# Priorities for the scan's chain and the merges of inverses in a hybrid encoder layer

## The chip, the core and the metric

The kernel runs on one core of a Trainium2 chip. A core has five engines that work side by side, each with a queue of its own that it takes strictly in order: TensorE (PE; its weight loads are shown as PEld), VectorE (DVE), ScalarE (ACT), GpSimd (POOL) and SyncE (SP). Transfers are issued from the queues of SP, POOL and ACT. The metric is the device time of one execution in microseconds (us). Three executions of the kernel before gave 2390.2, 2390.23 and 2392.87 us, a median of 2390.23.

## What is computed

One layer of a bidirectional hybrid encoder: a half-step feed-forward part, a mixing part and a second half-step feed-forward part, each with a residual, for 1024 tokens of width 1024. The mixing part has two groups of eight heads: a dilated attention and a recurrent delta rule that runs forward and backward over the tokens. The change touches the recurrence:

```python
def _rwkv7_step(state, inp):
    r, w, k, v, kk, kka = inp
    sa = jnp.einsum('dbhvk,dbhk->dbhv', state, kk)
    state = state * w[..., None, :] - sa[..., :, None] * kka[..., None, :] + v[..., :, None] * k[..., None, :]
    y = jnp.einsum('dbhvk,dbhk->dbhv', state, r)
    return state, y
...
for l in range(DEPTH):
    f = _swiglu(_rmsnorm(h, ffn1_pre_g[l]), ffn1_w_gate[l], ffn1_w_up[l], ffn1_w_down[l])
    h = h + 0.5 * _rmsnorm(f, ffn1_post_g[l])
    z = _rmsnorm(h, mix_pre_g[l]) @ w_in[l]
    y_att = _attention_group(z[..., :ATT_IN], cos, sin, attn_out_g[l])
    y_rwkv = _rwkv7_group(z[..., ATT_IN:], ...)
    mix = jnp.concatenate([y_att, y_rwkv], axis=-1) @ w_out[l]
    h = h + _rmsnorm(mix, mix_post_g[l])
    f = _swiglu(_rmsnorm(h, ffn2_pre_g[l]), ffn2_w_gate[l], ffn2_w_up[l], ffn2_w_down[l])
    h = h + 0.5 * _rmsnorm(f, ffn2_post_g[l])
```

## The kernel before

The recurrence is not run token by token. The tokens are cut into 8 blocks (`NB`) of two chunks of 64 tokens each, for both directions and all heads. Inside a chunk the recurrence becomes matrix products with the inverse of a triangular matrix, and only the chain of states goes from chunk to chunk. A block n passes four steps:

- `prep(n)`: loads the block's inputs (`in3`, `th_w`, `th_a`; SP, L182), forms scaled keys on DVE and ACT (`pr` L810 and L811, `bk` L814, L815 and L822, `th_a` L819 and L821), multiplies them on PE (`lp`, L830), masks the products on DVE (`lm`, L832), transposes keys (`bp` L838, copied to `bt` by ACT, L840) and writes parts of `lm` to a buffer in memory (`d_x`, SP, L846). Tile `in3` has one buffer.
- `solve(n)`: loads the right-hand side `X` from `d_x` (SP, L182) and inverts all 16-row triangles of the block at once, by 31 steps of two DVE instructions (`ttmp` L866, `Ti` L868); DVE copies the result into `X` (L870), and POOL writes `Ti` and `X` out (`d_t` L872, `d_tt` L873). POOL also clears the next `Ti` (L860, L862).
- `merge(n)`: POOL loads the small inverses back (`d11` L883, `tt` L886), and PE and ACT put inverses of full chunks together from them by two rounds of small products (`pa` L894, copy L896, `pb` L900, copy L902). `d11` has one buffer, `tt` two.
- `chain(n)`: for each of the two chunks, SP loads values into `uv` and into the state tile `sv` (L908; two buffers each), PE forms the right-hand side from the state (`xu` L941, copied to `xs` by ACT, L944), multiplies by the chunk's inverse (`xu` L952, copied to `uv` by ACT, L954), and from `uv` forms the new state (`st`, L949 and L959 to 960) and the output (`y`, L956 to 963). The profile names all sums that go through the helper `add` by its line, L937. DVE scales the state into the next `sv` (L968), and ACT copies `y` to `yb` (L970) and stores it (`y_d`, L972).

In the same loop, `project_attended` multiplies the output of the attention by the output weights: a load and a scaling on DVE (`yat` L1072), a transpose on PE (`yq` L1075), its high part on ACT (`yah` L1077) and remainder on DVE (`yal` L1078), 24 products for a tile on PE (`po`, L1064), and a copy and store on ACT (`yao` L1083). `out_weights` prepares the weights (`woh` L1054 on ACT, `wol` L1055 on DVE). After the loop, `finish_half` turns the outputs into rows of the mixing product (`f_y` L994, `yc` L995, `var` L1004, `bonus` L1011, `rstd` L1014, `gate` L1025).

The program is written in one sequence, and a scheduler then orders the instructions of each engine: among those that are ready by its model it takes the most urgent, and urgency is by default the place in the written sequence. Inside `tc.high_priority()` an instruction counts as more urgent than everything outside; with `offset=1000` it counts as written 1000 places earlier. What is fixed by this at build time is the order in each queue, and it is kept at run time even where an instruction waits.

## Time and profile before

| what | value |
|---|---|
| median of three executions | 2390.23 us |
| the profiled execution's own time | 2398.21 us |
| its span, from the first to the last instruction | 2396.4 us |
| PE busy | 2233.1 us (93%) |
| DVE busy | 1778.9 us (74%) |
| ACT busy | 1030.6 us (43%) |
| POOL busy | 572.8 us (24%) |
| TensorE clock, mean over the span | 0.951 |

The span is 1.8 us shorter than the execution's time; the rest lies around it. The loop of the scan takes the stretch from about 1269 to 1624 us: solve 0 has ended at 1268, and the last chain ends at 1623.6. Before it stand the first feed-forward part, the attention and the projections; behind it the finish, the mixing product and the second feed-forward part.

How the views are read: a busy share says how long an engine worked, not what it waited for. "DVE sv L968 <- PE st L937: 19.4, 9, 5.8" means that DVE stood idle for 19.4 us, nine times, 5.8 us at the longest, ahead of instructions of line 968 until PE's product for `st` was done. SPq is the queue of SyncE, that issues transfers. In a timeline, a row gives the start, the duration, the engine, line and operation, the tiles written and read, how many such instructions follow each other, and in brackets the idle time ahead of the row and what ended it. The granted clock is the share of full speed that TensorE was given.

### The profile page before, as it was taken

How to read it: one execution, taken by the hardware profiler on the slowest of the kernel's cores; microseconds unless marked ns; L12 is line 12 of the kernel's file. 1: busy time of each engine (PE TensorE's matmuls, PEld its weight loads, DVE VectorE, ACT ScalarE, POOL GpSimd, SP SyncE). 2: the span in 40 equal slices, each digit the busy share in tenths (PEclk: the TensorE clock that was granted, in tenths of full speed). 3: DMA queues.
4: the chain of work that ended last, by engine and by line, in shares of the span. 5: the costliest groups of instructions: out<-in, count | busy, mean ns of one | idle time of the engine just before them, and what ended most of it. 6: DMA issues, size and time to landing. Idle time of an engine off the chain costs nothing. (4 is left out here: it accounts for less than half of the span.)

```text
span 2396.4 us, 39330 instructions
## 1 busy us (share of the span) xinstructions
PE 2233.1 (93%) x14532; PEld 1801.5 (75%) x14532; DVE 1778.9 (74%) x2917; ACT 1030.6 (43%) x1918; POOL 572.8 (24%) x668
## 2 busy tenths in 40 slices
PE   6999999999999998999986788898989999999997
PEld 4788888788786676778775577775768888887886
DVE  8899999865675345666556766746889999997565
ACT  4422333354676304556544444445442233335452
POOL 6244344500000010111101121132234443442000
PEclk8999999999999998999995698789989999999999
DMA  5344544576743415322366766558534544448655
GB/s 155 110 172 150 171 158 156 181 257 194 227 152 133 161 50 157 84 71 72 91 173 174 177 157 166 146 173 268 186 107 172 180 150 167 164 152 268 194 189 180
DMA packets 359763, 386.03 MB, mean 161 GB/s; under 512 B 73618, under 2 KB 268050, under 8 KB 359572
## 3 DMA queue, kind: packets, MB, share of 16 engines
q1 hardware_dynamic: 311968, 284.82, 39.5%
q0 software_dynamic: 27248, 86.05, 9.7%
q10 hardware_dynamic: 20356, 12.66, 1.8%
q8 instruction: 114, 1.87, 0.3%
q14 instruction: 77, 0.63, 0.1%
HBM read 257.53 MB, written 125.89 MB: 160 GB/s over the span
## 5 line engine op out<-in xcount | busy, mean ns | idle before, releaser
L186 ACT ACTIVATE wh<-raw 128x512 fp32r<-128x512 f32 (+1 forms) x273 | 168.2, 627 | 261.8 <-DVE raw L62 94.0
L81 PE MATMUL gu<-xh,wh 128*128 128x512 f32 x704 | 277.2, 394 | 2.3 <-ACT wh L186 1.1
L187 DVE TENSOR_TENSOR wl<-raw,wh 128x512 fp32r<-128x512 f32 (+1 forms) x273 | 275.6, 1013 | 2.1 <-ACT wh L186 1.2
L81 PE MATMUL gu<-xh,wl 128*128 128x512 f32 x704 | 275.9, 392 | 0.0
L81 PE MATMUL gu<-xl,wh 128*128 128x512 f32 x704 | 275.7, 392 | 0.0
L415 PE MATMUL pd<-gl,gwh 128*128 128x512 f32 x616 | 240.5, 390 | 2.5 <-DVE gl L187 2.5
L415 PE MATMUL pd<-gh,gwh 128*128 128x512 f32 x616 | 239.6, 390 | 0.6 <-DVE row L86 0.6
L415 PE MATMUL pd<-gh,gwl 128*128 128x512 f32 x616 | 239.8, 389 | 0.0
L86 DVE TENSOR_TENSOR row<-gu,row 128x512 f32<-128x512 f32 x308 | 206.3, 682 | 26.1 <-PE gu L81 24.2
L187 DVE TENSOR_TENSOR gwl<-graw,gwh 128x512 fp32r<-128x512 f32 (+1 forms) x176 | 117.9, 672 | 128.4 <-ACT gwh L186 125.7
L116 POOL DMA_DIRECT2D d_hid<-row x154 | 84.7, 551 | 473.3 <-DVE row L114 446.2
L186 ACT ACTIVATE gwh<-graw 128x512 fp32r<-128x512 f32 (+1 forms) x176 | 101.4, 576 | 188.4 <-PE pd L415 157.5
L81 PEld LDWEIGHTS gu<-xh,wh 128*128 128x128 f32 x704 | 133.5, 190 | 31.6 <-ACT xh L186 2.0
L81 PEld LDWEIGHTS gu<-xl,wh 128*128 128x128 f32 x704 | 133.4, 189 | 27.5
L81 PEld LDWEIGHTS gu<-xh,wl 128*128 128x128 f32 x704 | 133.1, 189 | 27.6
L415 PEld LDWEIGHTS pd<-gl,gwh 128*128 128x128 f32 x616 | 115.6, 188 | 28.0 <-DVE gl L187 4.3
L415 PEld LDWEIGHTS pd<-gh,gwh 128*128 128x128 f32 x616 | 115.6, 188 | 25.3 <-DVE row L86 1.0
L415 PEld LDWEIGHTS pd<-gh,gwl 128*128 128x128 f32 x616 | 115.7, 188 | 23.8
L187 DVE TENSOR_TENSOR gl<-raw,gh 128x512 fp32r<-128x512 f32 x160 | 112.3, 713 | 17.0 <-ACT gh L186 16.7
L94 ACT ACTIVATE row<-row 128x512 f32<-128x512 f32 x44 | 27.8, 633 | 221.3 <-DVE row L86 217.5
L145 POOL TENSOR_TENSOR ws<-ws 128x512 f32<-128x512 f32 x88 | 114.2, 1298 | 1.1
L186 ACT ACTIVATE gh<-raw 128x512 fp32r<-128x512 f32 x160 | 98.0, 621 | 33.7 <-DMA raw<-in_ffn_w_down_dram 21.8
(354 smaller groups left out, 5345.7 us busy)
## 6 DMA issues: line engine op xcount, KB each, us to landing
d_hid<-row POOLq DMA_DIRECT2D x154, 256.0 KB, 2.4
graw<-d_hid SPq DMA_DIRECT2D x132, 256.0 KB, 3.0
raw<-in_ffn_w_gate_dram SPq DMA_DIRECT2D x88, 256.0 KB, 3.0
raw<-in_ffn_w_up_dram SPq DMA_DIRECT2D x88, 256.0 KB, 3.3
ws<-in_ffn_w_down_dram SPq DMA_DIRECT2D x88, 256.0 KB, 4.5
d_ws<-ws POOLq DMA_DIRECT2D x88, 256.0 KB, 2.3
raw<-d_ws SPq DMA_DIRECT2D x88, 256.0 KB, 2.7
raw<-in_ffn_w_down_dram SPq DMA_DIRECT2D x66, 256.0 KB, 3.6
```

The lines of the kernel that those rows point to most:

```text
L81: self.K.nc.tensor.matmul(ps, a[:, k, :], b[:, k, :], start=(k == 0 and i == 0), stop=(k == 3 and i == 2))
L86: add = lambda o, x: V.tensor_tensor(o, ps, x, op=OP.add)
L94: A.activation(y[:, 0], y[:, 0], AF.Silu)
L116: put = lambda n, y: G.dma_start(self.hid[n - 1, j // 2], y)
L145: G.tensor_tensor(o, a, b, op=OP.subtract)
L186: self.nc.scalar.activation(h, src, AF.Copy)
L187: (eng or self.nc.vector).tensor_tensor(l, src, h, op=OP.subtract)
L415: T.matmul(ps[x], a[:, ts], b, start=(m == 0 and k == 0), stop=(m == NM - 1 and k == 2))
```

## The change

The merge of every block but the first is written inside a priority of 1000 places, and the chain inside the highest priority. Nothing is added and nothing removed; the two lines that open these blocks shift later lines by two.

```diff
             for n in range(NB):
                 if n:
-                    self.merge(n, blk[n], sc, pm)
-                self.chain(n, blk.pop(n), sc, pc)
+                    with self.tc.high_priority(offset=1000):
+                        self.merge(n, blk[n], sc, pm)
+                with self.tc.high_priority():
+                    self.chain(n, blk.pop(n), sc, pc)
                 upto(n + 3)
                 for t in ([0, 1] if n == 0 else [n + 1] if n + 1 < NT else []):
                     self.project_attended(eo, sc, pe, t, WA, rs_a)
```

Every engine's order changes in the scan. Three places follow. First SyncE's queue at the solve of block 4, whose right-hand side is `X_13133`; `sv_13987` is a state tile of chain 3, `d_x0_152` the buffer through which block 4's `lm` goes. Before:

```order
L846 DMA d_x0_152<-lm_12991 32x16x32 x4
L908 DMA sv_13439<-d_vt_137 64x2x256 x2
L823 DMA d_kd0_140<-th_a_13543 128x4x128
L182 DMA X_13133<-d_x0_152 64x1024 x2
L908 DMA uv_13883<-d_vt_137 64x2x256 x2
L908 DMA sv_13886<-d_vt_137 64x2x256 x2
L182 DMA th_w_14089<-d_w0_110 128x4x128
L908 DMA uv_13984<-d_vt_137 64x2x256 x2
L182 DMA th_a_14091<-d_a0_116 128x4x128
L182 DMA yat_14304<-d_ya_101 128x512
L908 DMA sv_13987<-d_vt_137 64x2x256 x2
```

And now:

```order
L908 DMA uv_13883<-d_vt_137 64x2x256 x2
L823 DMA d_kd0_140<-th_a_13543 128x4x128
L182 DMA th_w_14089<-d_w0_110 128x4x128
L182 DMA th_a_14091<-d_a0_116 128x4x128
L908 DMA sv_13886<-d_vt_137 64x2x256 x2
L908 DMA uv_13984<-d_vt_137 64x2x256 x2
L846 DMA d_x0_152<-lm_12991 32x16x32 x4
L908 DMA sv_13987<-d_vt_137 64x2x256 x2
L182 DMA X_13133<-d_x0_152 64x1024 x2
```

The load of `X_13133` stood ahead of all values and states of chain 3 and now stands behind them, as does the store that it reads. At the start of the loop the same happens to the input `in3_11717` of block 1, second half; block 0's tiles are `uv_12212`, `sv_12215`, `sv_12218`, `uv_12296` and `sv_12299`. SyncE's difference there:

```order
-L182 DMA wor_12158<-in_w_out_dram 128x512
-L908 DMA uv_12212<-d_vt_137 64x2x256
-L182 DMA in3_11717<-d_rk_125 128x12x128
-L908 DMA uv_12212<-d_vt_137 64x2x256
+L908 DMA uv_12212<-d_vt_137 64x2x256 x2
 L908 DMA sv_12215<-d_vt_137 64x2x256 x2
 L908 DMA sv_12218<-d_vt_137 64x2x256 x2
 L908 DMA uv_12296<-d_vt_137 64x2x256 x2
-L908 DMA sv_12299<-d_vt_137 64x2x256
-L182 DMA wor_12164<-in_w_out_dram 128x512
-L908 DMA sv_12299<-d_vt_137 64x2x256
+L908 DMA sv_12299<-d_vt_137 64x2x256 x2
+L182 DMA in3_11717<-d_rk_125 128x12x128
+L182 DMA wor_12158<-in_w_out_dram 128x512
```

The input moved from behind the first load of values to behind the last load of a state. The third place is PE at merge 6 and the chunk of chain 6 behind it; `pa_15234` and `pb_15269` are the merge's products, `xu_15316` the chunk's right-hand side, `po_15526` and `po_15542` the attended products of the last tile. Before:

```order
L894 MATMUL pa_15234<-d11_15227,lm_14087 32x32 x32
L937 MATMUL st_15317<-sv_15083,ident_62 64x256 x4
L937 MATMUL y_15318<-pr_14098,sv_15083 64x64 x8
L937 MATMUL y_15318<-pr_14166,sv_15083 64x64 x8
L1064 MATMUL po_15526<-wol_12185,yah_15522 128x512
L1064 MATMUL po_15526<-woh_12184,yal_15523 128x512
L1064 MATMUL po_15526<-woh_12196,yah_15522 128x512
L900 MATMUL pb_15269<-tt0_11629,d11_15227 32x32 x32
L941 MATMUL xu_15316<-sv_15083,lm_14087 64x64 x16
```

And now:

```order
L894 MATMUL pa_15234<-d11_15227,lm_14087 32x32
L1064 MATMUL po_15542<-woh_12166,yah_15522 128x512
L1064 MATMUL po_15542<-wol_12167,yah_15522 128x512
L1064 MATMUL po_15542<-woh_12166,yal_15523 128x512
L1064 MATMUL po_15542<-woh_12178,yah_15522 128x512
L1064 MATMUL po_15542<-wol_12179,yah_15522 128x512
L941 MATMUL xu_15316<-sv_15083,lm_14087 64x64 x7
L1064 MATMUL po_15542<-woh_12178,yal_15523 128x512
L1064 MATMUL po_15542<-woh_12190,yah_15522 128x512
L900 MATMUL pb_15269<-tt0_11629,d11_15227 32x32 x32
```

All of `po_15526` has moved ahead of this merge, into and before chain 5, and only the 12 rows of `po_15542` are left beside chain 6, ahead of its first multiplication by the inverse; before, products of both stood in chain 6 up to its end. On POOL the loads of each merge (L883, L886) now stand ahead of the memset of the next `Ti` (L860, L862), and on PE merge 1 stands ahead of 12 attended products that it stood behind.

## The prediction

> **What bounds the kernel now.** The page comes first: where does TensorE (PE) lose time, and is its clock whole there?
>
> ```profile
> span 2396.4 us, 39330 instructions
> ...
> PE   6999999999999998999986788898989999999997
> ...
> PEclk8999999999999998999995698789989999999999
> ```
>
> A slice is 2396.4 / 40 = 59.9 us. The clock row is 9 nearly everywhere; slices 21 to 27 (1258 to 1677 us) hold its 5, 6, 7 and 8, and the PE row falls to 6 to 8 there. That is the scan of the recurrence, the stage that the change re-orders. Busy time in stretches of 100 us shows the same:
>
> ```profile
> 1200.00:1300.00 100.00, 75.84 (x578) 61.96 (x576) 58.91 (x128) 45.66 (x81) 12.42 (x19) 0.79 0.67 174
> 1300.00:1400.00 100.00, 75.91 (x923) 61.27 (x922) 71.35 (x224) 41.73 (x79) 15.61 (x26) 0.71 0.64 162
> 1400.00:1500.00 100.00, 87.19 (x1510) 72.51 (x1509) 65.97 (x172) 52.32 (x99) 15.66 (x26) 0.92 0.66 170
> 1500.00:1600.00 100.00, 91.89 (x1521) 74.31 (x1520) 68.35 (x224) 42.31 (x81) 21.91 (x33) 0.84 0.54 138
> ```
>
> Columns: stretch, length, busy us of PE, PE's weight loads, DVE, ACT and POOL, granted clock, DMA share, GB/s. No engine is full. PE at 76 to 92% runs partly on a reduced clock; DVE, which owns the solves, is at 59 to 71%. So the stage is bound by waits that go round between engines: prepare a block (PE and DVE), solve its 16-row inverses (DVE), merge them (PE and ACT), run the chain (PE, ACT, DVE). The table of waits for 1237 to 1640 us (total us, times, longest) says who waits:
>
> ```profile
> POOL d_t L872 <- DVE ttmp L866: 126.9, 2, 68.7
> ...
> DVE sv L968 <- PE st L937: 19.4, 9, 5.8
> DVE yal L1078 <- ACT yah L1077: 14.3, 4, 7.9
> ...
> DVE pr L810 <- DMA in<-d_rk: 8.0, 3, 6.1
> DVE ttmp L866 <- DMA X<-d_x: 7.4, 3, 4.6
> ...
> SPq L908 <- PE y L937: 59.7, 18, 10.8
> ```
>
> The first row is POOL idling until a solve is done, and costs nothing by itself. The four DVE rows do cost: the solver stands still for states, attended products and loads. The last row is the SyncE queue, held by a load of values into a state (sv) whose buffer the chain still reads. The last stage shows how such waits line up; here DVE, then PE:
>
> ```profile
> 1531.00 0.60 DVE L870 COPY X<-Ti 128x512 f32<-128x512 f32 x1
> ...
> 1551.04 0.60 DVE L870 COPY X<-Ti 128x512 f32<-128x512 f32 x1
> 1559.50 0.69 DVE L1078 TENSOR_TENSOR yal<-yq,yah 128x512 fp32r<-128x512 f32 x1 [7.86 <-ACT yah L1077]
> 1565.67 0.68 DVE L968 TENSOR_TENSOR sv<-st,gc 64x512 f32<-64x512 f32 x1 [3.33 <-PE st L937]
> ...
> 1584.03 0.60 DVE L870 COPY X<-Ti 128x512 f32<-128x512 f32 x1
> ```
>
> ```profile
> 1552.51 0.66 PE L1075 MATMUL yq<-ident,yat 128*128 128x128 f32 x4
> ...
> 1573.96 1.20 PE L894 MATMUL pa<-d,lm 32*32 32x32 f32 x64
> ...
> 1595.83 0.24 PE L894 MATMUL pa<-d,lm 32*32 32x32 f32 x2
> ...
> 1604.70 1.12 PE L995 MATMUL yc<-f_y,k_cen 128*128 128x512 f32 x2 [2.48 <-POOL f_y L994]
> ...
> 1623.55 1.13 PE L1025 MATMUL gate<-f_sg,g2w 128*128 128x256 f32 x4
> ```
>
> The L870 copies end the solves of blocks 5, 6 and 7 (at 1531.6, 1551.6, 1584.6). The solve of block 7 takes 33.0 us from the one before, because its owner waits 7.86 us for an attended product and 3.33 us for a state. The merges of blocks 6 and 7 start 22.4 us (1573.96 - 1551.6) and 11.2 us behind their solves, and chain 7 ends at 1623.55, where a finish unit's gate row takes PE.
>
> **The change part by part.** Nothing is added or removed; every term below is a shift. I walked the new order of every engine by hand with the durations of such groups (columns: total us, mean ns, idle before):
>
> ```profile
> L868 DVE TENSOR_TENSOR Ti<-Ti,ttmp 128x96 f32<-128x96 f32 (+20 forms) x248 | 61.1, 253 | 5.4
> ...
> L832 DVE TENSOR_TENSOR lm<-lp,k_tri 128x512 f32<-128x512 f32 x56 | 37.3, 684 | 15.5 <-PE lp L830 15.4
> ```
>
> *Part 1, the start.* SyncE now issues all values and states of block 0 before the input of block 1's second half, and the last of these waits for chain 0's first product. Now the input goes before them:
>
> ```profile
> 1270.44 0.78 SPq L182 DMA_DIRECT2D in<-d_rk  x1
> ...
> 1286.41 0.57 SPq L908 DMA_DIRECT2D sv<-d_vt  x1
> ```
>
> The held state load goes at 1286.41. In the new order PE's first chain product stands ahead of the preparation's, so I put that load near 1279 and the input near 1280, 10 us late; DVE's 6.1 us wait (its longest for `in`, in the table) is for this very load and hides none of it. But chain 0's rows, which held the preparations that follow, are then done, and the walk gives back 6 of the 10: **+4** for solve 1 (bounds 0 and +10).
>
> *Part 2, merge loads on POOL.* They stand ahead of the memsets for the next solve's tile:
>
> ```profile
> 1352.30 0.78 POOL L872 DMA_DIRECT2D d_t<-Ti  x1 [68.70 <-DVE ttmp L866]
> ...
> 1357.29 0.53 POOL L860 MEMSET Ti<- 128x512 f32 x1 [1.77 <-DMA d_t<-Ti]
> 1357.91 0.67 POOL L883 DMA_DIRECT2D d<-d_t  x1
> ```
>
> That alone is worth 0.53 us. On PE the merge of block 1 now also passes 12 attended products, ahead of which PE idles:
>
> ```profile
> 1354.84 0.79 PE L1064 MATMUL po<-woh,yah 128*128 128x512 f32 x1 [13.87 <-ACT woh L1054]
> ...
> 1370.54 0.31 PE L894 MATMUL pa<-d,lm 32*32 32x32 f32 x2
> ```
>
> Solve 1 ends at 1352.3 and its merge starts 18.2 us later, behind those products. The first merge load was issued at 1357.9, so the merge could start some 4 us after that (an estimate from the X load of part 3), near 1362. Chains 1 to 3 so run 10 to 15 us sooner. That moves no solve directly; it frees the blocks' buffers and the states.
>
> *Part 3, solve 4.* Its right-hand side (the X load) stands behind a state load that waits for chain 3. In the trace the X load goes first:
>
> ```profile
> 1426.75 1.10 SPq L182 DMA_DIRECT2D X<-d_x  x2
> ...
> 1450.73 1.24 SPq L908 DMA_DIRECT2D sv<-d_vt  x2
> ```
>
> ```profile
> 1434.23 0.19 DVE L866 TENSOR_TENSOR ttmp<-X,Ti 128x31 f32<-128x31 f32 x1 [4.56 <-DMA X<-d_x]
> ```
>
> The load of 1450.73 is the one it is now behind. It goes when chain 3's state product is read; with chain 3 some 15 us sooner that is about 1434 to 1435. From the X load's issue to the solve's first row the trace has 7.5 us (1434.23, after 4.56 us of idling), so solve 4 starts near 1441 to 1442, not 1434.2: **+7** (part 1's +4 goes into the same wait). Bounds: 0, and +25 if the state load goes at 1450.73 as now.
>
> *Part 4, preparations inside that wait.* While solve 4 waits, DVE has block 5's preparation ahead in its queue. One preparation is 8 masks of 0.684 us (the L832 row: 56 for seven blocks) and two each of the six products L810, L811, L814, L815, L821 and L822, whose rows have the shape and, to 0.01 us, the time of this one:
>
> ```profile
> L821 DVE TENSOR_TENSOR th_a<-th_a,in 128x512 f32<-128x512 f32 x13 | 9.0, 689 | 14.9 <-ACT th_a L819 14.9
> ```
>
> That is 8 x 0.684 + 12 x 0.689 = 13.7 us. Before, this was done after solve 4; the new order does nearly all of it first. Of the 13.7 I take 10, since its PE products also queue: **-10** (bounds 0 and -13.7). With part 3, solve 5 ends 3 us sooner; by the walk block 7's preparation is then also finished, where now DVE still does its last four masks after it:
>
> ```profile
> 1540.00 0.68 DVE L832 TENSOR_TENSOR lm<-lp,k_tri 128x512 f32<-128x512 f32 x1
> ...
> 1542.84 0.69 DVE L832 TENSOR_TENSOR lm<-lp,k_tri 128x512 f32<-128x512 f32 x1 [0.35 <-PE lp L830]
> ```
>
> These 4 x 0.684 = 2.7 us I take as **-2** (bounds 0 and -2.7). Solve 6 ends 5 us sooner, near 1546.5.
>
> *Part 5, the last three blocks.* The attended remainder that DVE waits for at 1559.50 needs PE's transposes of 1552.51. In the new order these stand right behind the first row of merge 5's second product, some 10 us sooner, and the states of chain 5 stand a dozen solver rows later on DVE. So solve 7 loses its 7.86 and 3.33 us and starts with solve 6's 5 us: it ends near 1568, not 1584.6, and no longer holds chain 7. The merge of block 6 starts when chain 5 ends, near 1564, 17.5 us after solve 6 in place of 22.4: **-5** (bounds 0 and -11, the gap that block 7 has). From merge 6 to the end of chain 7 PE now takes 1623.55 - 1573.96 = 49.6 us. It holds the chunks of chains 6 and 7 and the wait for solve 7 in between; without the 2.48 us wait, and with merge 7 loaded while chain 6 runs, the walk gives 45: **-4.5** (bounds -1, and -12).
>
> Behind chain 7 PE's order is row for row the same, so what is gained there is kept. The finish unit that runs inside chain 7 stays inside it.
>
> The sum: +7 - 10 - 2 - 5 - 4.5 = **-14.5 us**. The profiled execution took 2398.2 us (a span of 2396.4), so it would take 2383.7; that execution stands 8.0 us over the median of 2390.2, to which I apply the same shift: **2375.7 us**.
>
> **The clock.** Two stretches, one right behind waits, one dense:
>
> ```profile
> 1279.00:1300.00 21.00, 14.40 (x222) 13.30 (x222) 12.01 (x20) 11.25 (x21) 3.99 (x8) 0.50 0.60 161
> ...
> 1400.00:1436.00 36.00, 32.19 (x642) 26.92 (x641) 23.38 (x62) 20.85 (x40) 7.87 (x13) 1.00 0.74 181
> ```
>
> At 0.50, 14.4 us of PE work would be 7.2 at 1.00. The Trainium skill, page "TensorE: Matmul & The Clock Gate", section "What's actually happening", says that the clock has two states, half and whole, and that an idle window of about 3.4 us drops it to half until a busy one has passed. The trace agrees: PE idles 21 - 14.4 = 6.6 us in the first stretch and has 0.50 there, and 3.8 us of 36 in the second, with 1.00. This rule speaks against the change where it bunches work: chains that finish early leave one long gap in place of several small ones.
>
> **The rivals.**
>
> *A, the queue holds the solver (slower).* SyncE takes its loads in order. If the state load ahead of X of block 4 goes at 1450.7 as now, solve 4 starts 25 us late, not 7; its prepared work then covers 13.7 at best, and part 1's +4 counts too, as no slack is left: +25 - 13.7 + 4 - 2 - 5 - 4.5 = +3.8, and with no gain at the tail's first step (merge 6 late with it) +8.8: about 2399. With that loss it becomes slower than now from a release near 1450.7 - 8.8 = 1442. For it: 18 such waits, longest 10.8. Against: chain 3 can start with merge 3, which is now urgent. Chance 0.18.
>
> *B, nothing gained.* Solves are the clock of the stage: the row of L868 alone has 61.1 us, its partner as much, and the preparations 13.7 each. If parts 3 and 4 cancel, and chains 6 and 7 still wait for their solves as now, the shift is 0: 2390. For it: POOL's 126.9 us says that merges mostly wait for solves. Against: DVE is idle 30 to 40% of the stage. Chance 0.15.
>
> *C, the end gains more.* If chain 7 follows solve 7 by as much as now, 39 us, the 16.2 us of solve 7 and the 2.48 us wait both come out, and clocks whole in chains 5 to 7 give some 4 more (the half clock is priced above at 7.2 in 21 us): -23, or 2367. Chance 0.15.
>
> *D, bunched gaps.* Twice 7.2 us of half-speed work, ahead of merge 1 and at solve 4's wait, undo the gain: -14.5 + 14.4 = 0, about 2390. The window shows the price; nothing shows that the gaps grow. Chance 0.07.
>
> **How the numbers follow.** The forecast (-14.5) has 0.45. Its own range, parts 3 to 5 at half their bounds, is 2366 to 2385. A measurement of this kernel tells about 0.2%, 4.8 us, from no change. Faster by more: the forecast's 0.45 less 0.01, C's 0.15, and 0.05 of B's and D's spread, 0.64; slower by more: 0.13 of A and 0.03 of B, 0.16; the rest 0.20. The range of 2361 to 2398 takes in C and B and most of A.
>
> **What would show it.** Right: solve 7 (its L870 copy) 15 to 20 us sooner and no 7.9 us wait of L1078; merge 1 starting within 10 us of solve 1; the wait for the X load at solve 4 grown to some 10 us, yet solve 5 no later; chain 7's end 10 to 18 us sooner. Wrong: the state load ahead of X still going at about 1450 (A); solve 6 and merge 6 where they are (B); granted clock below 0.7 in two stretches of the scan (D). Wrong most of all would be chain 0 to 3 early and PE idle after them.

## The result, and the profile after

Four executions of the changed kernel took 2409.43 to 2419.17 us, median 2418.52; four of the kernel before, beside them, 2390.2 to 2394.91, median 2391.55. The ratio is 1.0102, 95% interval 1.0075 to 1.0129: **1% slower**, where the prediction had 0.6% faster and a range up to 2398. The profiled execution is the quickest of the four, 2409.43 us. The profile shown of before (2398.21 us) lies above its kernel's median. So the two traces differ by 11.2 us, the medians by 27.0; what lies between these is taken up under the hardware at the end.

The page of the changed kernel, with its clock row in 40 slices of 60.2 us:

```profile
span 2407.4 us, 39322 instructions
...
PEclk8999999999999998999996598899989999999999
```

In the scan 5 and 6 changed places, and two digits rose by one. The page can't show where 12 us went. The windows can (columns as in the prediction: busy time of PE, weight loads, DVE, ACT and POOL, granted clock, DMA share, GB/s). Here is the whole scan, from the end of solve 0 to the gate row; the second fence has the scan of the kernel before:

```profile
1267.50:1635.00 367.50, 302.14 (x4584) 242.34 (x4584) 231.32 (x658) 163.00 (x304) 72.08 (x107) 0.79 0.61 162
```

```profile
1268.00:1623.50 355.50, 294.77 (x4584) 242.28 (x4584) 227.21 (x659) 164.17 (x304) 71.81 (x107) 0.80 0.64 167
```

The same 4584 products take PE 7.4 us longer (302.14 against 294.77), and PE idles 65.4 us instead of 60.7. The mean clock of the scan is 0.79, where it was 0.80. The scan is 12.0 us longer, and that is the whole difference: solve 0 ends 0.6 us sooner than before, and from the gate row to the end it is 772.4 us here (2407.4 - 1635.05) and 772.9 before.

The ends of the solves 1 to 7, and the first rows of merge 6 and of the gate, from the timeline of the changed kernel, DVE and then PE:

```profile
1349.96 0.59 DVE L870 COPY X<-Ti 128x512 f32<-128x512 f32 x1
...
1391.61 0.59 DVE L870 COPY X<-Ti 128x512 f32<-128x512 f32 x1
...
1425.81 0.59 DVE L870 COPY X<-Ti 128x512 f32<-128x512 f32 x1
...
1484.61 0.59 DVE L870 COPY X<-Ti 128x512 f32<-128x512 f32 x1
...
1548.55 0.62 DVE L870 COPY X<-Ti 128x512 f32<-128x512 f32 x1
...
1570.59 0.60 DVE L870 COPY X<-Ti 128x512 f32<-128x512 f32 x1
...
1594.91 0.62 DVE L870 COPY X<-Ti 128x512 f32<-128x512 f32 x1
```

```profile
1589.67 1.19 PE L894 MATMUL pa<-d,lm 32*32 32x32 f32 x62
...
1635.05 1.13 PE L1025 MATMUL gate<-f_sg,g2w 128*128 128x256 f32 x4
```

The solves 1 to 4 of the kernel before:

```profile
1352.12 0.58 DVE L870 COPY X<-Ti 128x512 f32<-128x512 f32 x1
...
1374.32 0.62 DVE L870 COPY X<-Ti 128x512 f32<-128x512 f32 x1
...
1414.85 0.60 DVE L870 COPY X<-Ti 128x512 f32<-128x512 f32 x1
...
1459.98 0.60 DVE L870 COPY X<-Ti 128x512 f32<-128x512 f32 x1
```

Laid over each other at the end of solve 0, the changed kernel stands at -1.6 us at solve 1, +17.9 at solve 2, +11.6 at solve 3, +25.2 at solve 4, +18.2 at solve 5, +20.2 at solve 6, +11.5 at solve 7 and +12.1 at the gate row. (Solve 2, for one: 1392.20 - 1374.94 + 0.6.) So the loss comes in two steps, at solves 2 and 4; solves 3 and 5 give 6 and 7 us of them back, and the end 8 us.

**Solve 2.** It starts late, and then it waits. Its first row, of the kernel before and then of the changed one, with the wait behind it:

```profile
1341.16 0.40 DVE L866 TENSOR_TENSOR ttmp<-X,Ti 128x31 f32<-128x31 f32 x2 [0.40 <-DMA X<-d_x]
```

```profile
1352.86 0.19 DVE L866 TENSOR_TENSOR ttmp<-X,Ti 128x31 f32<-128x31 f32 x1
...
1373.21 0.27 DVE L866 TENSOR_TENSOR ttmp<-X,Ti 128x108 f32<-128x108 f32 x1
1381.87 0.69 DVE L1078 TENSOR_TENSOR yal<-yq,yah 128x512 fp32r<-128x512 f32 x1 [8.38 <-ACT yah L1077]
```

Counted from the end of solve 0, the first row comes 12.3 us later than before, and block 2's last mask (L832) 12.8 us later. Much of that is PE's: here are the products for the block's first masks, before and now.

```profile
1304.53 4.29 PE L830 MATMUL lp<-pr,bk 64*128 64x128 f32 x29
```

```profile
1316.48 1.60 PE L830 MATMUL lp<-pr,bk 64*128 64x128 f32 x18
```

These products stood ahead of chain 0's second chunk. Their last key (L822) was ready at 1304.2 then, and is at 1308.1 now; but all but four of them now stand behind that chunk and the first rows of chain 1, the last of which ends at 1316.55. The wait of 8.38 us inside the solve comes from PE too:

```profile
1363.60 1.91 PE L894 MATMUL pa<-d,lm 32*32 32x32 f32 x62 [0.39 <-DMA d<-d_t]
...
1371.13 1.12 PE L941 MATMUL xu<-sv,lm 128*64 128x64 f32 x14
...
1377.17 0.90 PE L1075 MATMUL yq<-ident,yat 128*128 128x128 f32 x3 [0.68 <-ACT yao L1083]
1378.01 1.91 PE L900 MATMUL pb<-tt,d 32*32 32x32 f32 x62
1379.85 0.47 PE L1075 MATMUL yq<-ident,yat 128*128 128x128 f32 x1
```

The solver's next step stands in DVE's queue behind a remainder of attended products, which needs four transposes of PE. Merge 1, chain 1 and attended products stand ahead of these, and 62 rows of merge 1's second product stand between the third and the fourth. It is the same kind of wait that held solve 7 before (7.86 us), at another place. In e1, a second profile of this order, both are there again (first row 12.6 us late, wait 7.93 us). PE also runs this stretch on a lower clock. The first row is of the changed kernel, the second of the one before:

```profile
1320.00:1380.00 60.00, 42.45 (x350) 32.43 (x348) 46.37 (x134) 26.09 (x48) 7.82 (x13) 0.50 0.61 162
```

```profile
1320.00:1380.00 60.00, 42.48 (x441) 34.04 (x440) 47.12 (x160) 24.10 (x44) 11.01 (x17) 0.66 0.73 181
```

PE is busy for the same 42.5 us and idle for the same 17.5, but gets through 350 products, not 441. The idle time lies otherwise: before, 13.87 us of it are one gap (the prediction's row of 1354.84); now the longest gap is this:

```profile
1343.45 3.32 PE L830 MATMUL lp<-pr,bk 64*128 64x128 f32 x22 [3.62 <-DVE bk L822]
```

**Solve 4.** SyncE, then DVE:

```profile
1434.69 2.65 SPq L846 DMA_DIRECT2D d_x<-lm  x4
1443.71 1.23 SPq L908 DMA_DIRECT2D sv<-d_vt  x2
1445.17 1.14 SPq L182 DMA_DIRECT2D X<-d_x  x2
```

```profile
1435.17 0.69 DVE L832 TENSOR_TENSOR lm<-lp,k_tri 128x512 f32<-128x512 f32 x1 [1.89 <-PE lp L830]
1450.45 0.19 DVE L866 TENSOR_TENSOR ttmp<-X,Ti 128x31 f32<-128x31 f32 x1 [14.58 <-DMA X<-d_x]
```

The queue stood still from 1437.3 to 1443.7 for the state load, and DVE did nothing at all for 14.58 us. It is easy to put the delay down to that queue, but block 4's preparation is late as well. The first fence has the products of its last two masks on PE, in the changed kernel; the second has the last two masks in the kernel before:

```profile
1432.00 0.49 PE L830 MATMUL lp<-pr,bk 64*128 64x128 f32 x4
...
1434.65 0.37 PE L830 MATMUL lp<-pr,bk 64*128 64x128 f32 x1
```

```profile
1418.69 1.29 DVE L832 TENSOR_TENSOR lm<-lp,k_tri 128x512 f32<-128x512 f32 x2 [0.44 <-PE lp L830]
```

On PE, rows of chain 2's second chunk stand ahead of these products, and the first rows of chain 3 between them. The last mask ends at 1435.86, where it ended at 1419.98: from the end of solve 0 it is 16.5 us late, and solve 4's first row 16.8. From the last mask to that row it takes 14.6 us now and took 14.3 before, when DVE filled most of this time with other work. In between, the trace has the store that X reads land 5.2 us behind the last mask, and X go 4.1 us after that landing (before 0.1); X itself then lands in 5.2 us, not 7.3. So at most 4.1 of the 16.8 us are the held queue's (8.6 in e1), and the late preparation makes the rest, 12.7 or more. Block 6 is like it: its last mask is 23.1 us late and solve 6's first row 26.0, with chain rows between the products on PE.

How many masks DVE had done when solve 4 began, and how many inside it, is told by the windows of line L832 alone (stretch, length, DVE's time and count on this line, clock), of after and of before:

```profile
1200.00:1450.40 250.40, 26.80 (x40) 0.76 0.63 166
1450.40:1484.90 34.50, 4.12 (x6) 0.90 0.38 107
```

```profile
1200.00:1434.20 234.20, 26.45 (x40) 0.79 0.67 170
1434.20:1460.00 25.80, 0.00 (x0) 1.00 0.42 125
```

Forty masks, those of blocks 0 to 4, stand ahead of solve 4 in both kernels. The new order put block 5's preparation not ahead of the solver's wait but behind its first row, in among its steps: solve 4 takes 34.8 us from its first row to its end, not 26.4.

The waits of the scan, 1237 to 1640 us (total, times, longest; compare the prediction's second table):

```profile
DVE sv L968 <- PE st L937: 28.7, 9, 8.6
DVE lm L832 <- PE lp L830: 23.4, 18, 4.5
DVE ttmp L866 <- DMA X<-d_x: 15.2, 2, 14.6
...
DVE yal L1078 <- ACT yah L1077: 9.7, 3, 8.4
```

Three of the four rows grew: states from 19.4 to 28.7, masks from 15.4 to 23.4, right-hand sides from 7.4 to 15.2. Attended remainders fell from 14.3 to 9.7.

### The profile page after: what moved, and what is told of

The parts are those of the page before. It is cut to its first block, busy times and chain, and to the rows that moved or that the text cites. A ratio compares the mean times of both kernels' runs of the same rounds, so it can differ in the third digit from the quotient of the medians.

```text
span 2407.4 us, 39322 instructions
## 1 busy us (share of the span) xinstructions
PE 2242.4 (93%) x14532; PEld 1801.8 (75%) x14532; DVE 1782.9 (74%) x2917; ACT 1029.8 (43%) x1918; POOL 572.8 (24%) x668
## 5 line engine op out<-in xcount | busy, mean ns | idle before, releaser
L187 DVE TENSOR_TENSOR gl<-raw,gh 128x512 fp32r<-128x512 f32 x160 | 112.4, 714 | 13.7 <-ACT gh L186 13.5
L94 ACT ACTIVATE row<-row 128x512 f32<-128x512 f32 x44 | 27.8, 632 | 216.8 <-DVE row L86 213.1
L186 ACT ACTIVATE gh<-raw 128x512 fp32r<-128x512 f32 x160 | 98.0, 621 | 28.6 <-DMA raw<-in_ffn_w_down_dram 18.3
```

Of the source, the lines that this page charges most:

```text
L94: A.activation(y[:, 0], y[:, 0], AF.Silu)
L186: self.nc.scalar.activation(h, src, AF.Copy)
L187: (eng or self.nc.vector).tensor_tensor(l, src, h, op=OP.subtract)
```

## The experiments

Each ratio is against the kernel before on the same chip, and can differ from the quotient of the two medians by 0.0014 (in e9). Medians of before were 2391.35 to 2394.52 us. Shifts of a solve are measured as above, from the end of solve 0, in one profile each.

### The change again, and its halves

**e1_again** is the changed kernel unaltered.

> The changed kernel as it is, to see how its executions spread (2409.4 to 2419.2 us so far) and where the 8 to 10 us between them lie. Queue theory (the load of X for solve 4 stands behind chain 3's state load in SyncE's queue, a wait of 14.6 us): X for solve 4 waits 13 us or more in every execution, and the median is 2409 to 2419. Engine theory (rows of chains and merges whose operands are late stand ahead of preparations and solver rows on PE and DVE): the same time; a slower execution shows longer waits of DVE for PE in solves 2 and 3, at a lower granted clock, and not at X.

2420.46 us, ratio 1.0113 [1.0088, 1.0138]. Its profiled execution took 2424.1 us, 14.7 more than the first profile of the same order. The median lies one us above the range that was expected, and X waits longer still. Here solve 3 stands at +13.3, solve 4 at +32.0, solve 6 at +30.1, the gate at +26.2:

```profile
1458.70 0.19 DVE L866 TENSOR_TENSOR ttmp<-X,Ti 128x31 f32<-128x31 f32 x1 [18.30 <-DMA X<-d_x]
```

The steps at solves 2 and 4 are there again, the second larger, and the preparations of blocks 2, 4 and 6 are 13.7, 18.3 and 32.5 us late. The end gave 3.9 us back, not 8.

**e2_chain_only** leaves the merges at their place in the sequence.

```diff
-                    with self.tc.high_priority(offset=1000):
-                        self.merge(n, blk[n], sc, pm)
+                    self.merge(n, blk[n], sc, pm)
```

> Only the chain is urgent, merges keep their default place. In this order the load of X for solve 4 is again issued ahead of chain 3's second state load, but block 1's input still behind block 0's states. Queue theory: the wait for X falls under 6 us and the time to 2390 to 2400 us. Engine theory: solves 2 and 3 stay 10 us late, and the time stays at 2405 us or more.

2415.16 us, 1.0094 [1.0069, 1.0119]. SyncE has the load of X for solve 4 ahead of the state load again (1443.54 and 1446.85 us). DVE's waits for X, 7.4 us before, are 0.0 in its table, and 22.7 us (2415.16 - 2392.49) are lost all the same. Solve 2 is at +9.1, but solve 3 at +0.7: the engine theory had the time right, and not that place. Block 4's preparation is 10.9 us late here too, and solve 4 starts 12.6 us late without any wait for X.

**e3_merge_only** leaves the chain at its place.

```diff
-                with self.tc.high_priority():
-                    self.chain(n, blk.pop(n), sc, pc)
+                self.chain(n, blk.pop(n), sc, pc)
```

> Only merges are urgent; SyncE's order at both places is that of before. Queue theory: no loss at solve 4 (wait for X under 6 us), 2382 to 2392 us. Engine theory: the merges' rows that wait for transfers stand ahead of preparations on PE, and cost at least 6 us: 2397 us or more.

2412.47 us, 1.009 [1.0063, 1.0118]. Urgent merges stand in PE's queue before the inverses that they multiply have been loaded. The table of waits (before: 1.0 us for the first of these rows, and 9.4 for the second):

```profile
ACT lm L928 <- PE pa L894: 27.1, 5, 17.4
...
PE pa L894 <- DMA d<-d_t: 22.7, 5, 12.6
```

This run has neither of the two steps: solve 2 stands at -9.0 and solve 4 at -4.3, and no preparation ends more than 5 us later than before (block 7's +0.7). Its loss comes behind them, with solve 7 at +13.4 and the gate at +19.1, just where the prediction looked for the gain.

So the halves alone cost 23 and 20 us, the two together 27: they overlap, and neither brings a gain that the other spoils.

### The SyncE queue

**e4_loads_default** is the change, with the loads of values and states put back to the numbers that they had before.

```diff
-        for par in range(2):
+        with self.tc.high_priority(offset=self.tc.cur_priority - self.p0):
+            for par in range(2):
...
+                self.p0 = self.tc.cur_priority
                 with self.tc.high_priority():
                     self.chain(n, blk.pop(n), sc, pc)
```

> The changed kernel, but the loads of values and states keep the urgency of the place where the chain is written; everything else of chain and merge stays urgent. X of solve 4 and block 1's input then go ahead of the state loads on SyncE. Queue theory: the wait for X falls from 14.6 to under 6 us and what the end of the scan gained shows: 2380 to 2395 us. Engine theory: 2405 us or more, with solves 2 and 3 as late as in the changed kernel (17 and 10 us).

2419.13 us, 1.0115 [1.0085, 1.0146]. The first row of solve 4 (the new lines shift those behind them by one):

```profile
1439.21 0.19 DVE L866 TENSOR_TENSOR ttmp<-X,Ti 128x31 f32<-128x31 f32 x1 [1.59 <-DMA X<-d_x]
```

The wait of 14.58 us is 1.59, and solve 4 ends where it did before (+0.2). But solve 5 is at +11.2 and the gate at +15.2. That looks like a proof that SyncE's queue made the delay. It is none: block 4's preparation is done 4.7 us sooner than before in this profile, and solve 4's first row follows its last mask by 16.9 us, more than the 14.6 of the changed kernel. X is still held by the queue, 8.0 us from the landing of its store, and the wait is short because DVE is busy meanwhile. And the total does not come back. Other waits came in its place: those of ACT for the merge (24.4 us, before 1.0), of PE for the merge's loads (14.6, before 9.4), and, once the loss was mostly there, one of solve 7 for its own X (11.0). So e4 leaves it open whether that queue costs elsewhere; e2, which never waits for X, shows that the loss does not need this wait.

### Which blocks

**e5_late5** makes only blocks 5 to 7 urgent.

```diff
-                if n:
+                if n > 4:
                     with self.tc.high_priority(offset=1000):
...
+                else:
+                    if n:
+                        self.merge(n, blk[n], sc, pm)
+                    self.chain(n, blk.pop(n), sc, pc)
```

> Merges and chains are urgent from block 5 on only; up to there every order is that of before. Feeding theory (a chain has slack until the last solves, a preparation has none, so urgent chains cost where preparations are still to come): the middle is as before, the end gains the 8 us that the changed kernel gained between solve 6 and the end of chain 7: 2380 to 2394 us. Fragile theory (the order of before happens to fit the waits, and any other order costs some 20 us): 2402 us or more.

2392.29 us, 1.0012 [0.9999, 1.0025]. Up to solve 3 its order is that of the kernel before. Yet in its profile solve 3 already ends 5.7 us sooner after solve 0 than in the other one:

```profile
1409.59 0.61 DVE L870 COPY X<-Ti 128x512 f32<-128x512 f32 x1
```

So two profiles of one order differ by that much in 140 us, and a shift below 6 us in one profile proves nothing.

**e6_early5** makes blocks 1 to 4 urgent (here and in the next four the other blocks are written as in e5_late5).

```diff
-                if n:
+                if 0 < n < 5:
...
```

> Merges and chains are urgent for blocks 1 to 4 only. Feeding theory: the loss is all here, solve 5 ends at least 12 us later after solve 0 than before, and the time is 2405 to 2425 us. Fragile theory: the same, so this run alone doesn't tell them apart; with the run that has the last blocks urgent it does.

2404.12 us, 1.0055 [1.0035, 1.0075]. Four neighbouring blocks cost about half of what all eight do. Solve 5, that was to be 12 us late by either theory, is at +2.1 in its profile and the gate at +1.9, so that profile doesn't show where the loss lies.

**e9_only0**, **e11_only1** and **e12_only3** make one block urgent.

```diff
-                if n:
+                if n == 0:
...
```

> Only chain 0 is urgent. With blocks 1 to 4 urgent the time was 13 us over before and with blocks 5 to 7 it was 1 over, against 27 for all; what is left, some 13 us, would be chain 0's if the parts add up. Feeding theory: chain 0 puts back the preparations of blocks 1 and 2 (block 1's second input behind the states of block 0): 2396 to 2406 us, solves 2 and 3 late. Rival (the parts don't add up; it is the whole chain of delays with a lower clock that makes the 27): 2388 to 2396 us.

2395.69 us, 0.9999 [0.9981, 1.0016]. Block 0's urgency costs nothing that can be measured; the time is in the rival's range.

```diff
-                if n:
+                if n == 1:
...
```

> Only merge 1 and chain 1 are urgent. Feeding theory: solve 2 is held up as in the changed kernel (it ended 41.7 us after solve 1 there, 22.2 us before), and 5 to 15 us of it are left at the end: 2396 to 2406 us. Rival (the delay of solve 2 is caught up, only the wait for X at solve 4 lasts): 2388 to 2395 us.

2396.1 us, 1.0002 [0.9985, 1.002]. Its solve 2 ends 31.3 us behind solve 1 (before 22.2, in the changed kernel 41.7), and by solve 4 nothing of that is left: it ends 7 us sooner than in the kernel before, and the gate comes 4.8 us sooner. The 5 to 15 us that the feeding theory expected at the end are not there.

```diff
-                if n:
+                if n == 3:
...
```

> Only merge 3 and chain 3 are urgent. Their state load stays behind X of solve 4 on SyncE, so the wait for X stays short. Feeding theory: what feeds solves 4 and 5 is put back a little: 2391 to 2402 us. Rival (only the queue of SyncE matters in the middle): 2388 to 2394 us.

2395.4 us, 1.0008 [0.9991, 1.0025]. Nothing that can be measured.

**e10_not_first** makes all blocks but the first urgent.

```diff
-                if n:
+                if n > 0:
...
```

> All merges and chains are urgent but chain 0. Additive: 2402 to 2410 us, as blocks 1 to 4 alone. Rival: 2412 to 2422 us, near the changed kernel, as chain 0 matters little.

2414.08 us, 1.0089 [1.0064, 1.0114]. Its solve 2 is 109.1 us behind solve 0 (before 106.8), so the step at solve 2 is nearly absent, and the loss stays at 21 us. The profile is of its slowest execution, and there the loss comes at solve 4: it starts 11.0 us late, takes 43.1 us in place of 26.4 and ends at +27.8, with a wait for X of 1.9 us only.

So the cost is not that of any of the blocks tried alone (0, 1 and 3), nor of the wait at solve 2. It doesn't add up either: blocks 1 to 4 make 13 us and 5 to 7 make 1, and all seven 21. Block 1's delay alone is caught up by solve 4. That in a row of four or more each next block is disturbed in its turn is an argument from these totals; no run follows it block by block.

### Did the preparations starve?

The next theory was that urgent chains keep the preparations from PE and DVE, so that the solver runs dry; then preparations (and solves, which stand in the same call) that are urgent too should bring the time back.

**e13_prep_too**: the change, and preparations and solves in the highest priority.

```diff
-                upto(n + 3)
+                with self.tc.high_priority():
+                    upto(n + 3)
```

> The changed kernel, and the preparations and solves that are written in the loop get the highest priority too, so that only the attended products are left behind. Feeding theory (the loss comes from preparations put back behind urgent chains and merges): most of the 27 us comes back, 2388 to 2402 us, solve 5 within 8 us of before. Rival (urgent chains and merges cost by themselves, by their waits at the heads of the in-order queues): 2408 us or more.

2428.64 us, 1.015 [1.0128, 1.0172].

**e14_prep_above**: preparations and solves in the highest, chain and merge at 1000 places.

```diff
-                with self.tc.high_priority():
+                with self.tc.high_priority(offset=1000):
                     self.chain(n, blk.pop(n), sc, pc)
-                upto(n + 3)
+                with self.tc.high_priority():
+                    upto(n + 3)
```

> Preparations and solves in the loop get the highest priority, chains and merges the 1000 places only. Feeding theory: as the run before or better, 2386 to 2400 us. Rival: 2404 us or more.

2421.63 us, 1.0114 [1.0096, 1.0133].

**e7_prep_first**: only preparations and solves urgent, chain and merge as before.

```diff
-                upto(n + 3)
+                with self.tc.high_priority(offset=1500):
+                    upto(n + 3)
```

> The reverse: merges and chains as before, preparations and solves written inside a priority of 1500 places, so that they pass chains and merges. Feeding theory: solve 5 ends no later than before, the chains bunch behind it: 2385 to 2400 us. Fragile theory: 2405 us or more, with solve 5 late.

2396.53 us, 1.002 [1.0001, 1.004]. None of the three gains; put beside urgent chains, urgent preparations win nothing back. Two of them say little about the theory, though, since their profiles show no earlier preparations: in e13 block 2's last mask is still 15.4 us late and block 7's 15.8, and in e7 block 4's is 9.0 us later than before. Only e14 tests it in part. There block 2 is 16.3 us late, but blocks 4 and 6 are done at -1.5 and +0.7, and solve 7 ends at +4.5. The gate still comes at +17.1: what the solves got back was lost between the last solve and the end of chain 7. So late preparations are seen in the changed kernel, but that putting them on time brings back the total is not shown.

### Attended products put off

**e8_attended_late**: chain and merge as before, attended products counted 1000 places later.

```diff
-                for t in ([0, 1] if n == 0 else [n + 1] if n + 1 < NT else []):
-                    self.project_attended(eo, sc, pe, t, WA, rs_a)
+                with self.tc.high_priority(offset=-1000):
+                    for t in ([0, 1] if n == 0 else [n + 1] if n + 1 < NT else []):
+                        self.project_attended(eo, sc, pe, t, WA, rs_a)
```

> Merges, chains, preparations and solves as before; the attended products alone are written 1000 places later, so that chains and preparations pass them. Feeding theory: nothing that feeds a solve is put back, solver waits for attended products go: 2380 to 2396 us. Fragile theory: 2405 us or more.

2395.94 us, 1.002 [1.0003, 1.0036]. The scan is 14.4 us shorter in its profile, and the stage behind it 10 us longer (783 against 772.9): the work put off fell due there.

**e15_att_mid**: the same for the blocks 0 to 4 alone.

```diff
+                with self.tc.high_priority(offset=-1000 if n < 5 else 0):
```

> Nothing is urgent; the attended products of blocks 0 to 4 of the loop are written 1000 places later, those of the last tiles stay where they were. With all of them later the scan was 14 us shorter in its profile and the stage behind it 10 us longer, since products were left for it. Feeding theory: the scan keeps some 10 us and the rest loses nothing: 2378 to 2388 us. Rival (the 14 us are the spread of one profile): 2388 to 2396 us.

2390.74 us against 2394.52, ratio 0.9982 [0.9966, 0.9999]. This is the best order found, about 0.2% below the kernel before, in the range of the rival and not in that of the feeding theory. One interval of eighteen that just misses 1 can be luck, so a gain is not shown. The idea was to put off what does not feed the solver, as long as the scan still has gaps to take it up.

### Two more

**e16_lm_pool**: the change, with the chain's four copies of keys into `lm` (L928) on GpSimd. They overwrite what the merge's first products read, and ACT waited 14.7 us for that (before 1.0).

```diff
-                A.copy(lm[half(par), par, d, :, :, 0:64],
+                nc.gpsimd.tensor_copy(lm[half(par), par, d, :, :, 0:64],
```

> The changed kernel with the chain's four copies into lm (line 928) moved from ACT to GpSimd. In the changed kernel ACT stands still for 15 to 18 us ahead of these copies until PE has done merge products, with preparations' rows behind them; 1 us before. Theory (urgent rows whose operands are late stand at the heads of the in-order queues, ACT's above all): 8 us or more come back, 2412 us or less. Rival (no single queue's head is the loss, it sits in all of them): 2413 to 2425 us.

2438.51 us, 1.0196 [1.0169, 1.0224]. Above both expected ranges. It says that this move is worse. It does not say that ACT's wait was harmless, since the scheduler ordered the whole scan anew.

**e17_dose300** and **e18_dose100** lower both priorities.

```diff
-                    with self.tc.high_priority(offset=1000):
+                    with self.tc.high_priority(offset=300):
...
-                with self.tc.high_priority():
+                with self.tc.high_priority(offset=300):
```

> Merges and chains are both written 300 places earlier, in place of 1000 and of the head of the program. Theory (the loss grows with how far rows are pulled ahead of their operands): between before and the changed kernel, 2396 to 2410 us. Rival (any urgency over preparations costs the whole): 2413 us or more.

2474.58 us, 1.0343 [1.0315, 1.0372], far worse than the full dose.

```diff
-                    with self.tc.high_priority(offset=1000):
+                    with self.tc.high_priority(offset=100):
...
-                with self.tc.high_priority():
+                with self.tc.high_priority(offset=100):
```

> Merges and chains are both written 100 places earlier. Theory: close to before, 2388 to 2398 us. Rival: 2400 us or more.

2413.7 us, 1.0081 [1.0052, 1.011]. Neither run fits the theory that the loss grows with the distance; a middling urgency is the worst of the three. In e18's profile the loss also lies elsewhere: the scan is 6.1 us longer than before, and the stage behind it 14.0.

### One picture of all

The longest waits of DVE inside the scan in three dear orders (those that cost 20 us or more), from the timelines of e2, e10 and e13, and at what they stand:

```profile
1427.98 0.69 DVE L821 TENSOR_TENSOR th_a<-th_a,in 128x512 f32<-128x512 f32 x1 [8.88 <-ACT th_a L819]
```

```profile
1446.26 0.69 DVE L1072 TENSOR_TENSOR yat<-yat,rs 128x512 f32<-128x512 f32 x1 [11.26 <-DMA yat<-d_ya]
```

```profile
1611.08 1.41 DVE L968 TENSOR_TENSOR sv<-st,gc 64x512 f32<-64x512 f32 x2 [14.98 <-PE st L937]
```

A key from ACT, an input of the attended products, a state at the end: with the X of the changed kernel, four orders with four different longest waits. What they have in common shows in the scan as a whole, here of e1_again and e10, and then of two cheap orders, e5 and e15:

```profile
1270.30:1652.00 381.70, 312.33 (x4585) 249.52 (x4585) 231.38 (x659) 163.12 (x304) 72.59 (x107) 0.76 0.59 156
```

```profile
1270.00:1654.00 384.00, 315.43 (x4586) 251.40 (x4587) 232.01 (x662) 163.67 (x304) 70.71 (x106) 0.76 0.59 154
```

```profile
1268.00:1617.20 349.20, 288.74 (x4551) 235.24 (x4552) 229.54 (x658) 164.68 (x304) 70.88 (x107) 0.81 0.65 170
```

```profile
1267.50:1612.60 345.10, 289.66 (x4584) 235.09 (x4585) 226.06 (x658) 163.76 (x304) 72.39 (x107) 0.83 0.66 174
```

DVE, ACT and POOL are busy for the same time in all four, within 6 us. PE's products take 312 and 315 us at a clock of 0.76 in the dear orders, 289 and 290 at 0.81 and 0.83 in the cheap ones; PE's idle time (length less busy) is 69 and 69 us against 60 and 55. So between these four most of the difference is PE on a lower clock, and the rest idling. That split is not general: measured the same way, PE is busy for 304.5 us and idle for 69.2 in e2, and 300.9 and 73.6 in e3 (before 294.8 and 60.6), so there idling is as much of it or more. The profiles show both together; no run here separated which brings on which.

## Why the prediction was wrong

By its own steps, counted from the end of solve 0, in the two profiles that it compares and in the second profile of the changed order:

| step | predicted | measured | again (e1) |
|---|---|---|---|
| parts 1 and 2: to the end of solve 3 | +4 | +11.6 | +13.3 |
| part 3: from there to the first row of solve 4 | +3 | +5.2 | +9.0 |
| part 4: from there to the end of solve 6 | -12 | +3.4 | +7.9 |
| part 5: solve 6 to merge 6 | -5 | -3.9 | -3.0 |
| part 5: merge 6 to the end of chain 7 | -4.5 | -4.2 | -0.9 |
| sum | -14.5 | +12.1 | +26.2 |

The prediction lets part 1's +4 go into part 3's wait, so that solve 4 starts at +7; the first two rows split that +7. Each measured figure is a difference of rows. Part 3's, for one: solve 4 begins 16.2 us later (1450.45 - 1434.23), that is 16.8 from solve 0, less the 11.6 that were there at solve 3. Two profiles of one order can differ by 6 us within 140 (e5), and these two differ by 14 at the end, so single terms below that prove little; the sum of the first three rows, +20 and +30 where -5 was forecast, is far outside.

**Part 1** had +4 for solve 1, and nothing of it came (-1.6, and -1.3 in e1). It costs the end nothing (e9 at 0.9999).

**Part 2** held the first failed step: chains 1 to 3 sooner "moves no solve directly". Merge 1 did start sooner, at 1360.84, 10.3 us behind solve 1 and just outside the 10 that the prediction asked for (before it was 17.8 us; the prediction's 18.2 takes 1352.3 for solve 1's end, which is 1352.7). But the rows that urgent chains and merges passed on PE were not all idle work. Among them were the products that the next preparations need: block 2's last mask came 12.8 us late and block 4's 16.5, and solves 2 and 4 began 12.3 and 16.8 us late. The transposes of the next attended tile stood among them too, and DVE's queue had their remainder in the middle of solve 2: 8.38 us. I had walked that very chain (attended transposes, ACT, DVE remainder, solver) for solve 7, and took it as a wait that would go, without asking where the new order puts it next. The chains did not come 10 to 15 us sooner either: merge 3 starts at 1437.27, 1.3 us sooner than before.

**Part 3** read SyncE's order rightly, and the state load does stand ahead of X and goes late, at 1443.71 and not at 1434 to 1435. But it took the load for the cause and block 4's preparation as on time. The preparation was 16.5 us late, and solve 4 followed it by about as much as before (14.6 us, before 14.3); of these the held queue has at most 4.1. That the total does not hang on the wait for X is what e2 shows.

**Part 4** held the second failed step: "While solve 4 waits, DVE has block 5's preparation ahead in its queue". It does not: 40 masks stand ahead of solve 4 in both kernels, DVE idled 14.58 us without a break, and the preparation came in among the solver's steps. Its 10 us were counted as cover for a wait in which nothing could run. The 2 us behind it fell with it: from solve 4's first row to solve 6's end it takes 3.4 us longer, and 7.9 in e1, not 12 less. Block 6's preparation, the next that chain rows held up on PE, is part of that.

**Part 5** came out in the first profile: 18.5 us from solve 6 to merge 6 (forecast 17.5), and 45.4 from merge 6 to the gate (forecast 45). The 7.86 us wait of L1078 at solve 7 went in both profiles (none above 1.1 us is left there). But the second has only -3.0 and -0.9, so the near agreement is partly luck. Three urgent blocks alone gain nothing that can be measured (e5, 1.0012), so even the right part is smaller than the spread of a profile.

**The rivals.** A had the right sign, and the state load was late as it said (release 1443.7, above its turning point of 1442). That this is the smaller part of solve 4's delay is told by the preparation's end, and that the loss doesn't need it by e2. B had solve 6 unmoved; it came 20 us later. C's sooner end did not come. D's price was half there: PE's products take 7.4 us longer, and 60 us ran at 0.50 in place of 0.66. Its mechanism, gaps bunched into longer ones, was not: the one long gap of 13.87 us was in the kernel before, and in the changed one the same 17.5 us of idle time lie in pieces of at most 3.62 us. The rule cited from the Trainium skill ("TensorE: Matmul & The Clock Gate", "What's actually happening") has a busy window of about 3.4 us bring back the whole clock. The trace does not agree: by its rows, whose ends are modelled, PE is busy without a gap for 12.9 us here, and the granted clock stays at 0.50.

```profile
1363.60:1376.50 12.90, 12.90 (x117) 8.78 (x117) 9.09 (x30) 5.87 (x10) 0.00 (x0) 0.50 0.38 94
```

The kernel before has such a stretch too, 12.1 us from 1358.8 at 0.51. What holds the clock down there, no run here shows.

**Where it is settled and where not.** Shown: the changed order loses in the scan alone (behind the gate row it takes 772.4 us, 770.2 in e1, and 772.9 before). Chains alone and merges alone each cost 20 us or more; blocks 0, 1 and 3 alone and the last three together cost nothing measurable, four neighbours about 13, seven 21. In both profiles of the changed order the preparations of blocks 2, 4 and 6 end 13 to 33 us late, with chain rows ahead of their products on PE, and their solves start late with them. Neither the wait for X (e2, e3, e10) nor the step at solve 2 (e3, e10) is needed for a loss of 20 us. Open: how much of the 27 us the late preparations make. e3 loses 20 us with preparations within 5 us of before, and e14 17 us at the gate with two of the three on time. Open too is why the delays of a single urgent block are caught up and those of a row of blocks are not. No one wait was found whose removal gives the time back.

## What to carry to other kernels

Urgency moves waiting, and each queue is in order: before a chain is raised, list what it passes on every engine, and who waits for that, in the next rounds too and not only where the old wait stood. Work counts as cover for a wait only if it stands ahead of the waiting row in the same queue, which can be read off by counting rows ahead of it. The bracket of a wait names what ended it last, not what was late: measure from the end of the work before it (here the last mask) to the waiting row, in several orders, before a queue is blamed. And where a program reads 20 us apart from one execution to the next, a sum of terms of 2 to 7 us from one trace can't carry a sign.

## What the hardware showed unasked

The time of one order goes with its clock. Over 88 executions of the kernel before, 2383.7 to 2404.1 us, the mean clock was 0.945 to 0.958; at 0.948 the mean time was 2398.3, at 0.951 2391.8. The order of e10 ranged from 2401.57 to 2431.89. Eight executions of the changed order had a median clock of 0.9445 and a median of 2418.5 us. At an equal clock it is slower all the same: 11 us at 0.948 (one execution, 2409.43 beside that mean of 2398.3), 19 at 0.947 (one, 2417.03 beside 2397.96) and 18 at 0.945 (two, 2418.5 beside 2400.6). By an estimate from the 88, a line through them has a slope of about 1.4 us for 0.001 of clock, which makes 9 us of the step from 0.951 to 0.9445. So some 9 of the 27 us go with the mean clock; whether as cause or as effect isn't shown. That lower mean is the scan's own: 0.76 in place of 0.80 over 382 of e1_again's 2422 us is worth 0.006 of the mean, and its mean is 0.944 against 0.951. Why one and the same order runs 10 to 20 us apart, or at another clock, from one execution to the next, no run here tells.
